# Hybrid decoder trunk on one core: the first layer's normalised input made from a second, already transposed copy of x

## The chip, the core and the metric

One Trainium2 chip, one core. The metric is the device time of one execution in microseconds. In the text, PE is TensorE, PEld its weight loads, DVE VectorE, ACT ScalarE, POOL GpSimd, and SP the engine whose queue issues most DMAs.

## What is computed

Two decoder layers on x, 256 tokens by 1024, batch 1. Each layer normalises x, projects it to ten groups of 512 columns, runs three branches on them (block attention, a gated linear recurrence, attention to 256 memory tokens), multiplies by a SiLU gate and adds the output projection to x.

```python
for l in range(DEPTH):                                   # 2
    h = rms_norm(x, norm_g[l])
    proj = h @ w_in[l]                                   # 1024 x 5120
    q_a, k_a, v_a, q_h, f_h, i_h, q_m, z = jnp.split(proj, split_points, axis=-1)
    qa, ka = rope(rms_norm(q_a)), rope(rms_norm(k_a))    # 8 heads x 64
    o_a = moba_attention(qa, ka, v_a)
    o_h = rms_norm(hgrn2_chunkwise(q_h, f_h, i_h, lb_all[l]), hgrn_o_norm[l])   # 4 heads x 128
    kv_m = rms_norm(mem, mem_norm_g[l]) @ w_mem_kv[l]
    k_m, v_m = jnp.split(kv_m, 2, axis=-1)
    o_m = memory_attention(rms_norm(q_m), rms_norm(k_m), v_m)                   # 4 heads x 128
    y = jnp.concatenate([o_a, o_h, o_m], axis=-1) * jax.nn.silu(z)
    x = x + y @ w_out[l]
```

## The kernel before

**Matmuls in three passes.** Each f32 operand is split into a high half (rounded to fp32r) and a low half (the rest), and a product is high x high, high x low and low x high. Weights come in chunks of 128 x 1024 from HBM, 60 per layer. For each chunk SP loads `wr`, ACT makes `wh` (L207 or L211) and DVE makes `wl` (L221 or L225); there are 4 buffers of `wr` and 3 each of `wh` and `wl`. Chunks 0 to 7 are the memory's keys and values, 8 to 11 the forget gates (one head of 128 columns each), 12 to 15 the recurrence's queries, 16 to 19 the attention's keys (KA), 20 to 23 the recurrence's input (IH), 24 to 27 the attention's queries (QA), and so on to the output projection.

**The normalised input.** The projections need x with its 1024 columns on the partitions: `hT`, eight tiles of 128 columns by 256 tokens, each with a high and a low half side by side (`hTh`, `hTl`). `g_norm` makes it: ACT squares the rows of `xs` with a sum, DVE and POOL turn the sum into a factor per token `r`, DVE scales the rows (`xn`, L473), PE transposes sixteen blocks of 128 x 128 (L481) into a side tile `sd`, and ACT and DVE take the halves out of it with the gain `gT` (L489, L490). For layer 0 this runs beside the memory's key and value matmuls (`group_kv`), whose operand `mT` comes from HBM in columns. `group_a` then computes the forget gates with `hT` as the moving operand; ACT copies the second half of the accumulator out as `al` and DVE adds it to the first as `as` (`g_sum`, L351 and L352).

**Work beside it in this stage.** `g_mem_r` squares the memory's rows (`memr`, L448) for its factor `rm`. `g_km` copies the key accumulators out as `kn` (DVE the first, ACT the second), ACT squares them (`sq`), DVE reduces the squares (L618), and POOL makes the factor `rk` after eight mask steps `mk` (L597) which need `xf`; `xf` lies in a buffer of `sq`. DVE then scales `kn` (L648). `g_vm` takes the value accumulators out as `vmh` (ACT) and `vml` (DVE). `g_setup` makes the rotation tables in many small DVE steps (`rt`), the last of which feeds one sine on ACT (`sc`, L561), behind a load of the sine's table. In the recurrence DVE computes `hQ` and ACT copies the last of it to `hQb` (L811). `g_ih` copies the IH accumulators out on ACT (L735).

**What sets the order.** Each piece of vector work is a generator that a `step()` per half chunk of matmuls moves on. From the recorded program a list scheduler with a timeline of its own sets the final order on each engine, fixed when the kernel is built; `tc.keep_in_program_order` and `tc.issue_after` hold an instruction in place. Accumulators have 4 buffers, side tiles 4.

Of the kernel before, what the change touches and what calls it, by code (L numbers as in the profile page):

```python
# [18 lines left out]
OP = mybir.AluOpType  # L19
# [25 lines left out]
@with_exitstack  # L45
def hymba_kernel(ctx: ExitStack, tc: tile.TileContext, x, mem, mem_t, positions, w_in, w_out, w_mem_kv,
                 gains, moba_g, out):
# [152 lines left out]
    def h_to(n):  # L200
        while st["h"] < min(n, len(chunks)):
            i = st["h"]
            whs[i] = sb.tile([128, 1024], F32R, name="wh", tag="wh", bufs=WH_BUFS)
            g = chunks[i][2]
            if g is None:
                with behind("ACT"):
                    nc.scalar.copy(whs[i], raws[i])  # L207
            else:
                for sl in parts(i):
                    with behind("ACT"):  # L210
                        nc.scalar.activation(whs[i][:, sl], raws[i][:, sl], AF.Copy, scale=gT[:, g:g + 1])  # L211
            st["h"] += 1

    def l_to(n):
        while st["l"] < min(n, len(chunks)):
            i = st["l"]
            wls[i] = sb.tile([128, 1024], F32R, name="wl", tag="wl", bufs=WL_BUFS)
            g = chunks[i][2]
            if g is None:
                with behind("DVE"):  # L220
                    nc.vector.tensor_tensor(wls[i], raws[i], whs[i].bitcast(F32), op=OP.subtract)  # L221
            else:
                for sl in parts(i):
                    with behind("DVE"):
                        ins = nc.vector.scalar_tensor_tensor(wls[i][:, sl], in0=raws[i][:, sl], scalar=gT[:, g:g + 1],  # L225
                                                             in1=whs[i][:, sl].bitcast(F32),
                                                             op0=OP.mult, op1=OP.subtract)
# [65 lines left out]
    def group_kv(th, tl, km, vm):  # L293

        acc = [[acc_tile() for _ in range(2)] for _ in range(2)]

        def part(c, g):
            i = c + c0
            wH, wL = whs[i][:, g * 512:(g + 1) * 512], wls[i][:, g * 512:(g + 1) * 512]
            for t in range(2):  # L300
                ts = slice(t * 128, (t + 1) * 128)
                mm(acc[g][t], th[:, c, ts], wH, c == 0, False)
                mm(acc[g][t], tl[:, c, ts], wH, False, False)
                mm(acc[g][t], th[:, c, ts], wL, False, c == 7)

# [12 lines left out]
        for c in (6, 7):  # L318
            part(c, 0)
            if c == 7:  # L320
                spawn(km(acc[0]))
            slot(False)
        for c in (6, 7):
            part(c, 1)
            fin()
            if c == 7:
                spawn(vm(acc[1]))
            slot(True)
# [116 lines left out]
    def g_mem_r():  # L445
        ss = small("ssm", 2)
        for t in range(2):
            nc.scalar.activation(memr[t], memr[t], AF.Square, accum_out=ss[:, t:t + 1])  # L448
        rel("P", 2)
# [10 lines left out]
    def g_norm(l):  # L460
# [10 lines left out]
        yield  # L471
        for t in range(2):
            nc.vector.tensor_scalar(xn[t], xs[:, t], r[:, t:t + 1], None, op0=OP.mult)  # L473
        yield 3
        for kp in range(4):
            yield from room("sd")
            pt = side_tile()
            for j in range(2):
                k = kp * 2 + j
                for t in range(2):  # L480
                    ins = nc.tensor.transpose(pt[:, j * 256 + t * 128:j * 256 + (t + 1) * 128],  # L481
                                              xn[t][:, k * 128:(k + 1) * 128], ident)
                    if l == 0:
                        tc.keep_in_program_order(ins)
            for j in range(2):
                k = kp * 2 + j
                c = GR_NORM + 8 * l + k
                src = pt[:, j * 256:(j + 1) * 256]
                nc.scalar.activation(hTh[:, k], src, AF.Copy, scale=gT[:, c:c + 1])  # L489
                nc.vector.scalar_tensor_tensor(hTl[:, k], in0=src, scalar=gT[:, c:c + 1],  # L490
                                               in1=hTh[:, k].bitcast(F32), op0=OP.mult, op1=OP.subtract)
# [123 lines left out]
    def sumsq(dst, acc, n):  # L615
        sq = sb.tile([128, 512], F32, name="sq", tag="sq", bufs=2)
        nc.scalar.activation(sq, acc, AF.Square)
        nc.vector.tensor_reduce(dst, heads(sq, n), AX.X, OP.add)  # L618
# [46 lines left out]
    def g_vm(l, acc):  # L665
# [4 lines left out]
        for t in range(2):  # L670
            nc.scalar.activation(vmh[:, t], acc[t], AF.Copy, scale=rm[:, t:t + 1])
            nc.vector.scalar_tensor_tensor(vml[:, t], in0=acc[t], scalar=rm[:, t:t + 1], in1=vmh[:, t].bitcast(F32),
                                           op0=OP.mult, op1=OP.subtract)
        T["vm"] = vmh, vml
# [692 lines left out]
```

## Time and profile before

| | us |
|---|---|
| median of 3 runs | 391.02 (390.81 to 393.14) |
| the profiled execution, device time | 390.31 |
| its span, first to last instruction | 388.5 |
| PE busy | 383.0 |
| DVE busy | 320.6 |
| ACT busy | 247.9 |
| POOL busy | 84.7 |
| granted TensorE clock | 0.999 |

The page gives busy times, the chain of work that ended last, and groups by line. In rows of the timeline the columns are the start in us from the span's start, the length in us of the merged row, the engine, line, operation, output<-inputs, shape, and how many instructions (xN); in brackets stands how long the engine was idle ahead of it and which instruction ended that. Matmuls are pipelined, so the next one starts before the last one's length is over; the cost of one is the step from start to start.

### The profile page before, as it was taken

What the parts mean: (1) busy time and instruction counts of PE and PEld (TensorE: products, weight loads), DVE (VectorE), ACT (ScalarE), POOL (GpSimd) and SP (SyncE); (2) the same over time, 40 slices, a digit from 0 to 9 for tenths busy, and PEclk for the clock granted to TensorE, in tenths of its full rate; (3) what the DMA queues carried; (4) which work ended last, traced back from release to release, by engine and by line L of the source; (5) the groups of instructions that cost most, each with busy time, mean ns of one, the idle gap of its engine ahead of it and who ended that gap; (6) DMA issues with size and microseconds to landing.
All of it is one profiled execution on the core that took longest, in us unless ns stands there. A gap on an engine that the chain in (4) does not pass through costs nothing.

```text
span 388.5 us, 6794 instructions
## 1 busy us (share of the span) xinstructions
PE 383.0 (99%) x2455; PEld 318.6 (82%) x2455; DVE 320.6 (83%) x621; ACT 247.9 (64%) x414; POOL 84.7 (22%) x129
## 2 busy tenths in 40 slices
PE   8999999999999999999999999999999999999996
PEld 5888887888788888778888888888888888877885
DVE  5789899999659999877576789899696799997663
ACT  5988755567768749473376666445765894885540
POOL 3014300525103523400000040014061063342000
PEclk9999999999999999999999999999999999999999
DMA  7986595539534999975454558636665189998512
GB/s 268 421 300 217 177 310 165 168 116 324 180 102 160 274 283 347 323 221 183 162 197 162 188 192 250 237 111 205 232 208 172 54 264 278 343 313 257 183 42 108
DMA packets 26241, 84.48 MB, mean 217 GB/s; under 512 B 3552, under 2 KB 5984, under 8 KB 26208
## 3 DMA queue, kind: packets, MB, share of 16 engines
q1 hardware_dynamic: 22304, 71.31, 55.1%
q0 software_dynamic: 3616, 12.59, 10.3%
q8 instruction: 19, 0.31, 0.3%
q10 hardware_dynamic: 288, 0.15, 0.1%
q14 instruction: 14, 0.11, 0.1%
HBM read 74.60 MB, written 9.44 MB: 216 GB/s over the span
## 4 chain that ended last, share of the span: by engine, by line
PE 97%; DMA 1%; DVE 0%; SPq 0%; ACT 0%; issue 0%; DVEq 0%
PE acc L268 69%; PE acc L1253 17%; PE sd L268 6%; PE sd L272 4%; DMA wr<-in_w_mem_kv_dram 1%; PE sd L481 1%; PE sd L1139 0%; PE sd L1009 0%; SPq L171 0%; ACT wh L211 0%; DVE xs L1287 0%; DVE xs L1294 0%; DVEq L1294 0%
## 5 line engine op out<-in xcount | busy, mean ns | idle before, releaser
L207 ACT CAST wh<-wr 128x1024 fp32r<-128x1024 f32 x96 | 100.8, 1051 | 69.3 <-PE acc L268 50.9
L221 DVE TENSOR_TENSOR wl<-wr,wh 128x1024 fp32r<-128x1024 f32 x96 | 116.8, 1217 | 26.2 <-ACT wh L207 26.0
L268 PE MATMUL acc<-wh,hT 128*128 128x512 f32 x384 | 122.9, 394 | 0.0
L268 PEld LDWEIGHTS acc<-wh,hT 128*128 128x128 f32 x384 | 71.5, 188 | 15.8 <-issue 0.7
L268 PE MATMUL acc<-wl,hT 128*128 128x512 f32 x192 | 75.6, 394 | 0.0
L268 PE MATMUL acc<-hT,wh 128*128 128x512 f32 x256 | 64.8, 392 | 0.0
L268 PEld LDWEIGHTS acc<-hT,wh 128*128 128x128 f32 x256 | 46.0, 189 | 8.5 <-ACT kn L631 0.4
L268 PEld LDWEIGHTS acc<-wl,hT 128*128 128x128 f32 x192 | 36.1, 188 | 7.3
L225 DVE SCALAR_TENSOR_TENSOR wl<-wr,gT,wh 128x1024 fp32r<-128x1024 f32 (+1 forms) x29 | 31.1, 1097 | 9.5 <-ACT wh L211 9.4
L1253 PE MATMUL acc<-wl,yh 128*128 128x512 f32 (+1 forms) x96 | 37.4, 390 | 0.0
L1253 PE MATMUL acc<-wh,yl 128*128 128x512 f32 (+1 forms) x96 | 37.2, 388 | 0.0
L268 PEld LDWEIGHTS acc<-hT,wl 128*128 128x128 f32 x256 | 34.9, 190 | 2.5
L211 ACT ACTIVATE wh<-wr,gT 128x1024 fp32r<-128x1024 f32 (+1 forms) x29 | 28.3, 1001 | 12.8 <-PE acc L1253 5.0
L268 PE MATMUL acc<-hT,wl 128*128 128x256 f32 x256 | 35.7, 282 | 0.0
L1253 PE MATMUL acc<-wh,yh 128*128 128x512 f32 (+1 forms) x96 | 33.6, 394 | 0.2
L268 PE MATMUL acc<-wh,mTh 128*128 128x512 f32 x64 | 25.0, 394 | 0.7 <-ACT mTh L422 0.4
L268 PE MATMUL acc<-wh,mTl 128*128 128x512 f32 x64 | 24.8, 390 | 0.0
L974 POOL TENSOR_TENSOR rka<-msa,pw 128x8 f32<-128x8 f32 x4 | 9.9, 2476 | 58.2 <-DVE msa L973 58.2
L1060 ACT ACTIVATE P<-P,nba,rq 128x128 f32<-128x128 f32 (+1 forms) x32 | 17.1, 536 | 8.3 <-DVE nba L1054 8.3
L1253 PEld LDWEIGHTS acc<-wh,yh 128*128 128x128 f32 x96 | 18.0, 188 | 5.0 <-issue 1.7
L1253 PEld LDWEIGHTS acc<-wl,yh 128*128 128x128 f32 x96 | 18.0, 188 | 4.0 <-DVE wl L225 0.7
L1253 PEld LDWEIGHTS acc<-wh,yl 128*128 128x128 f32 x96 | 18.0, 188 | 3.7
(219 smaller groups left out, 588.2 us busy)
## 6 DMA issues: line engine op xcount, KB each, us to landing
wr<-in_w_in_dram SPq DMA_DIRECT2D x80, 512.0 KB, 4.2
wr<-in_w_out_dram SPq DMA_DIRECT2D x24, 512.0 KB, 5.9
wr<-in_w_mem_kv_dram SPq DMA_DIRECT2D x15, 512.0 KB, 4.4
there<-blk POOLq DMA_DIRECT2D x4, 768.0 KB, 5.8
PT<-there POOLq DMA_DIRECT2D x16, 192.0 KB, 4.7
there<-blk POOLq DMA_DIRECT2D x6, 512.0 KB, 5.5
there<-blk SPq DMA_DIRECT2D x4, 512.0 KB, 2.8
P<-there POOLq DMA_DIRECT2D x16, 128.0 KB, 6.3
```

The lines of the kernel that those rows point to most:

```text
L207: nc.scalar.copy(whs[i], raws[i])
L211: nc.scalar.activation(whs[i][:, sl], raws[i][:, sl], AF.Copy, scale=gT[:, g:g + 1])
L221: nc.vector.tensor_tensor(wls[i], raws[i], whs[i].bitcast(F32), op=OP.subtract)
L225: ins = nc.vector.scalar_tensor_tensor(wls[i][:, sl], in0=raws[i][:, sl], scalar=gT[:, g:g + 1], in1=whs[i][:, sl].bitcast(F32), op0=OP.mu ...
L268: nc.tensor.matmul(o, lhsT=a, rhs=b, start=s, stop=e)
L272: tc.keep_in_program_order(nc.tensor.matmul(o, lhsT=a, rhs=b, start=s, stop=e))
L481: ins = nc.tensor.transpose(pt[:, j * 256 + t * 128:j * 256 + (t + 1) * 128], xn[t][:, k * 128:(k + 1) * 128], ident)
L974: nc.gpsimd.tensor_tensor(r[:, t8], ms[:, t8], pw[:, :8], op=OP.pow)
L1060: nc.scalar.activation(P[:, i, kc[t]], P[:, i, kc[t]], AF.Exp, bias=nb[:, c:c + 1], scale=rq[:, r:r + 1], accum_out=sm[:, c:c + 1])
L1253: ins = nc.tensor.matmul(a, lhsT=y, rhs=wt[:, cs], start=n == (0 if to is None else nk - 2) and j == 0, stop=n == nk - 1 and j == 2)
```

## The change

The host passes a second copy of x, `x_t`, in which each partition holds one column index and the tokens lie in strips of 32. It is loaded to a tile `xT` (128 x 2048), two DMAs of 512 KB. In layer 0 the factor `r` is spread along 128 columns (`rc`), two matmuls against the identity turn it into a row of factors on all partitions (`rb`), and DVE multiplies each of the eight column tiles of `xT` by gain and factor; ACT and DVE then take the high and low halves four tiles at a time. Layer 1 keeps the transposes. `xT` shares its memory with the two halves of the recurrence's gated output, which become one tile `y`. In `group_kv`, in both layers, the matmuls of the last two chunks are kept in program order, so the key accumulators end first. `in_turn` then chains instructions of layer 0 on DVE and on ACT.

```diff
+    def in_turn(*names):
+        for a, b in zip(names, names[1:]):
+            tc.add_manual_dep(N[b].ins, N[a].ins.name,
+                              mybir.DependencyInfo(mybir.DependencyClass.NoSync, mybir.DependencyReason.DATA),
+                              reason="in_turn")
...
-        def part(c, g):
+        def part(c, g, pinned=False):
...
-                mm(acc[g][t], th[:, c, ts], wH, c == 0, False)
-                mm(acc[g][t], tl[:, c, ts], wH, False, False)
-                mm(acc[g][t], th[:, c, ts], wL, False, c == 7)
+                for a, b in ((th, wH), (tl, wH), (th, wL)):
+                    ins = nc.tensor.matmul(acc[g][t], lhsT=a[:, c, ts], rhs=b, start=c == 0 and (a, b) == (th, wH),
+                                           stop=c == 7 and (a, b) == (th, wL))
+                    if pinned:
+                        tc.keep_in_program_order(ins)
...
         for c in (6, 7):
-            part(c, 0)
+            part(c, 0, True)
...
+    xT = sb.tile([128, 8, 8, 32], F32, name="xT", tag=f"y{H_}", bufs=1)
+    for t in range(2):
+        load(xT[:, 4 * t:4 * t + 4].rearrange("p q k i -> p (q k i)"),
+             dram(x_t, t * 128 * D, [[D, 128], [1, D]]))
     for t in range(2):
         load(memr[t], dram(mem, t * 128 * D, [[D, 128], [1, D]]))
...
+        if l == 0:
+            rc = sb.tile([128, 2, 128], F32, name="rc", tag="sq", bufs=2)
+            nc.vector.tensor_copy(rc, r[:, :, None].to_broadcast([128, 2, 128]))
+            yield 2
+            rb = side_tile()
+            for t in range(2):
+                mm_row(rb[:, t * 128:(t + 1) * 128], rc[:, t], ident)
+            rb3 = rb[:, :256].rearrange("p (q i) -> p q i", i=32)
+            yield
+            for k in range(8):
                 c = GR_NORM + 8 * l + k
+                N["xT", k] = nc.vector.scalar_tensor_tensor(xT[:, :, k], in0=xT[:, :, k], scalar=gT[:, c:c + 1], in1=rb3,
+                                                            op0=OP.mult, op1=OP.mult)
+                if k % 4 == 3:
+                    ks = slice(k - 3, k + 1)
+                    src = xT[:, :, ks].rearrange("p q k i -> p k q i")
+                    hi, lo = (a[:, ks].rearrange("p k (q i) -> p k q i", i=32) for a in (hTh, hTl))
+                    N["hTh", k // 4] = nc.scalar.copy(hi, src)
+                    N["hTl", k // 4] = nc.vector.tensor_tensor(lo, src, hi.bitcast(F32), op=OP.subtract)
             rel()
+        else:
...
         group_a(hT, lambda h, a: g_f(l, h, a))
+        if l == 0:
+            in_turn(*(("xT", k) for k in range(8)), ("hTl", 0), ("kn", 0), ("hTl", 1),
+                    ("wl", 8), ("wl", 9), ("vml", 0), ("vml", 1), ("wl", 10))
+            in_turn(("memr", 0), ("hTh", 0), ("hTh", 1), ("kn", 1), ("wh", 8), ("memr", 1), ("wh", 9),
+                    ("vmh", 0), ("vmh", 1), ("wh", 10), ("knsq", 0))
...
+    def strips(a):
+        return a.reshape(2, 4, 32, 8, 128).transpose(0, 4, 1, 3, 2)
...
+        "x": v["x"], "x_t": strips(v["x"]), "mem": v["mem"], "mem_t": columns(v["mem"]).reshape(128, 4, 512).transpose(1, 0, 2),
```

The scheduler moves other instructions as well. First the DMA queue of SP at the start, before and after:

```order
L171 DMA wr<-in_w_mem_kv_dram 128x1024 x3
L171 DMA memr<-in_mem_dram 128x1024 x2
L171 DMA wr<-in_w_in_dram 128x1024 x4
L171 DMA pos_i<-in_positions_dram 128x2
L171 DMA mg<-in_moba_g_dram 128x256
```

```order
L179 DMA wr<-in_w_mem_kv_dram 128x1024 x3
L179 DMA xT<-in_x_t_dram 128x1024 x2
L179 DMA memr<-in_mem_dram 128x1024 x2
L179 DMA wr<-in_w_in_dram 128x1024 x3
L179 DMA pos_i<-in_positions_dram 128x2
L179 DMA mg<-in_moba_g_dram 128x256
```

The two loads of `xT` stand ahead of the memory's rows, and one weight load fewer stands ahead of the positions.

Next DVE while the first forget gates run, up to the reduction of the memory keys' squares (`ssk`):

```order
L221 TENSOR_TENSOR wl<-wr,wh 128x1024
L521 CAST pf<-pos_i 128x2
L672 SCALAR_TENSOR_TENSOR vml<-acc,rm,vmh 128x512
L221 TENSOR_TENSOR wl<-wr,wh 128x1024
L524 TENSOR_TENSOR rt<-pf,fr 128x16
L672 SCALAR_TENSOR_TENSOR vml<-acc,rm,vmh 128x512
L618 TENSOR_REDUCE ssk<-sq 128x4 x2
```

```order
L362 TENSOR_TENSOR as<-acc,al 128x256
L566 TENSOR_SCALAR rt<-rt 128x16
L567 TENSOR_SCALAR rt<-rt 128x16
L572 SCALAR_TENSOR_TENSOR rt<-rt 128x16 x2
L706 SCALAR_TENSOR_TENSOR vml<-acc,rm,vmh 128x512
L565 TENSOR_SCALAR rt<-rt 128x16
L706 SCALAR_TENSOR_TENSOR vml<-acc,rm,vmh 128x512
L566 TENSOR_SCALAR rt<-rt 128x16
L229 TENSOR_TENSOR wl<-wr,wh 128x1024
L567 TENSOR_SCALAR rt<-rt 128x16
L651 TENSOR_REDUCE ssk<-sq 128x4 x2
```

Before, the reduction follows the second `vml` at once, behind the `wl` of the second and third gate heads; now the first head's sum `as` and four steps of the rotation tables stand ahead of the first `vml`, and the `wl` of the third head between the second `vml` and the reduction.

Last ACT at the end of the IH group, ahead of the copies of its accumulators (`ih`):

```order
L207 CAST wh<-wr 128x1024 x2
L811 COPY hQb<-hQ 128x16x32
L207 CAST wh<-wr 128x1024
L561 ACT_TABLE_LOAD
L561 ACTIVATE sc_164<-rt 128x32
L735 COPY ih<-acc 128x512
```

```order
L215 CAST wh<-wr 128x1024 x2
L849 COPY hQb<-hQ 128x16x32
L594 ACT_TABLE_LOAD
L594 ACTIVATE sc_167<-rt 128x32
L215 CAST wh<-wr 128x1024
L769 COPY ih<-acc 128x512
```

The table load and the sine stand ahead of the weight's cast now; the copy `ih` still comes behind all three.

More of the change, by code (lines that the diff above doesn't have):

```diff
@@ L45, in hymba_kernel @@
 @with_exitstack
-def hymba_kernel(ctx: ExitStack, tc: tile.TileContext, x, mem, mem_t, positions, w_in, w_out, w_mem_kv,
+def hymba_kernel(ctx: ExitStack, tc: tile.TileContext, x, x_t, mem, mem_t, positions, w_in, w_out, w_mem_kv,
                  gains, moba_g, out):
@@ L206, in h_to @@
                 with behind("ACT"):
-                    nc.scalar.copy(whs[i], raws[i])
+                    N["wh", i] = nc.scalar.copy(whs[i], raws[i])
             else:
@@ L447, in g_mem_r @@
         for t in range(2):
-            nc.scalar.activation(memr[t], memr[t], AF.Square, accum_out=ss[:, t:t + 1])
+            N["memr", t] = nc.scalar.activation(memr[t], memr[t], AF.Square, accum_out=ss[:, t:t + 1])
         rel("P", 2)
@@ L616, in sumsq @@
         sq = sb.tile([128, 512], F32, name="sq", tag="sq", bufs=2)
-        nc.scalar.activation(sq, acc, AF.Square)
+        N["sq"] = nc.scalar.activation(sq, acc, AF.Square)
         nc.vector.tensor_reduce(dst, heads(sq, n), AX.X, OP.add)
@@ L629, in g_km @@
         kn = sb.tile([128, 2, 512], F32, name="kn", tag="qk", bufs=1)
-        nc.vector.tensor_copy(kn[:, 0], acc[0])
-        nc.scalar.copy(kn[:, 1], acc[1])
+        N["kn", 0] = nc.vector.tensor_copy(kn[:, 0], acc[0])
+        N["kn", 1] = nc.scalar.copy(kn[:, 1], acc[1])
         yield
@@ L670, in g_vm @@
         for t in range(2):
-            nc.scalar.activation(vmh[:, t], acc[t], AF.Copy, scale=rm[:, t:t + 1])
-            nc.vector.scalar_tensor_tensor(vml[:, t], in0=acc[t], scalar=rm[:, t:t + 1], in1=vmh[:, t].bitcast(F32),
-                                           op0=OP.mult, op1=OP.subtract)
+            N["vmh", t] = nc.scalar.activation(vmh[:, t], acc[t], AF.Copy, scale=rm[:, t:t + 1])
+            N["vml", t] = nc.vector.scalar_tensor_tensor(vml[:, t], in0=acc[t], scalar=rm[:, t:t + 1],
+                                                         in1=vmh[:, t].bitcast(F32), op0=OP.mult, op1=OP.subtract)
         T["vm"] = vmh, vml
@@ L766, in y_tiles @@
         if f"y{br}" not in T:
-            T[f"y{br}"] = [sb.tile([128, 4, 256], F32R, name=f"y{c}{br}", tag=f"y{c}{br}", bufs=1) for c in "hl"]
+            if br == H_:
+                y = sb.tile([128, 2, 4, 256], F32R, name=f"y{br}", tag=f"y{br}", bufs=1)
+                T[f"y{br}"] = [y[:, 0], y[:, 1]]
+            else:
+                T[f"y{br}"] = [sb.tile([128, 4, 256], F32R, name=f"y{c}{br}", tag=f"y{c}{br}", bufs=1) for c in "hl"]
         return T[f"y{br}"]
@@ L1348 @@
     laid = {
-        "x": v["x"], "mem": v["mem"], "mem_t": columns(v["mem"]).reshape(128, 4, 512).transpose(1, 0, 2),
+        "x": v["x"], "x_t": strips(v["x"]), "mem": v["mem"], "mem_t": columns(v["mem"]).reshape(128, 4, 512).transpose(1, 0, 2),
         "positions": v["positions"].reshape(2, 128).T,
```

50 lines of the change are left out of this document (26 added, 24 removed).

## The prediction

> **What bounds the kernel now.** The share of busy time comes first, then the chain that ended last.
>
> ```profile
> span 388.5 us, 6794 instructions
> PE 383.0 (99%) x2455; PEld 318.6 (82%) x2455; DVE 320.6 (83%) x621; ACT 247.9 (64%) x414; POOL 84.7 (22%) x129
> PE 97%; DMA 1%; DVE 0%; SPq 0%; ACT 0%; issue 0%; DVEq 0%
> ```
>
> PE works 383.0 of 388.5 us, and 97% of the chain is PE. Next I ask who makes PE wait; the answer is three rows, all in the first 7 us.
>
> ```profile
> PE sd L268 <- DVE dm L396: 1.0, 1, 1.0
> PE acc L268 <- ACT mTh L422: 0.4, 1, 0.4
> PE acc L268 <- ACT wh L211: 0.3, 1, 0.3
> ```
>
> So from then until the output leaves, PE never stands still. Any matmul taken out shortens the run by its own length, but only if every operand is ready that much sooner. An engine that has no slack at one place turns the gain into a wait there, and PE never makes up a wait. Which engine has no slack? The stretches say VectorE (columns: stretch and length, then busy time and instructions of PE, PEld, DVE, ACT, POOL, then clock, DMA share, GB/s).
>
> ```profile
> 60.00:70.00 10.00, 10.00 (x165) 7.91 (x164) 10.00 (x33) 5.00 (x7) 0.70 (x1) 1.00 0.42 136
> 100.00:120.00 20.00, 20.00 (x119) 16.26 (x118) 12.97 (x48) 15.55 (x32) 0.00 (x0) 1.00 0.35 116
> ```
>
> DVE is busy all of the 10 us from 60 to 70, and 12.97 of 20 us after 100. What is late must be late before 100.
>
> **The change on PE.** The sixteen transposes of layer 0 stand here:
>
> ```profile
> 21.77 1.03 PE L481 MATMUL sd<-ident,xn 128*128 128x128 f32 x8
> 22.56 0.71 PE L268 MATMUL acc<-wl,mTh 128*128 128x512 f32 x2
> 23.11 1.04 PE L481 MATMUL sd<-ident,xn 128*128 128x128 f32 x8
> 23.90 0.47 PE L268 MATMUL acc<-wh,mTh 128*128 128x512 f32 x1
> 24.21 0.39 PE L268 MATMUL acc<-wh,mTl 128*128 128x512 f32 x1
> 24.44 0.39 PE L268 MATMUL acc<-wh,mTh 128*128 128x512 f32 x1
> ```
>
> An ordinary matmul follows the last by 0.23 us (24.21 to 24.44). From 21.77 to 24.21 there are three of them, 0.68 us, so the transposes take 2.44 - 0.68 = 1.76 us. The two matmuls that spread the factor (rb) have no row. Bounds: the same shape as a transpose, 0.10 us each (21.77 to 22.56 for eight), or at most an ordinary 512-column one, 0.23 us. The nearest are plain matmuls of f32 tiles, 128x128:
>
> ```profile
> 110.41 1.27 PE L268 MATMUL sd<-ih,hST 128*128 128x128 f32 x10
> 111.52 0.39 PE L268 MATMUL sd<-ih,hX 128*128 128x128 f32 x2
> ```
>
> Ten in 1.11 us, 0.11 each; I take 0.22 for the pair. **PE's work falls by 1.54 us** (1.30 to 1.56).
>
> [...]
>
> **The head of the forget gates.** They begin at 29.46; without the 1.54 at 27.92. Can the columns be ready?
>
> ```profile
> 14.63 0.90 SPq L171 DMA_DIRECT2D memr<-in_mem_dram x2
> DMA to landing us min/median/max: 6.0/6.4/6.8
> 17.98 1.42 DVE L473 TENSOR_SCALAR xn<-xs,rx 128x1024 f32<-128x1024 f32 x2 [0.84 <-POOL rx L470]
> 19.31 3.67 DVE L225 SCALAR_TENSOR_TENSOR wl<-wr,gT,wh 128x1024 fp32r<-128x1024 f32 x3
> 25.77 1.26 DVE L490 SCALAR_TENSOR_TENSOR hT<-sd,gT,hT 128x256 fp32r<-128x256 f32 x3
> 28.51 0.89 POOL L574 COPY rtA<-mg 128x96 f32<-128x96 f32 x4 [2.27 <-DMA mg<-in_moba_g_dram]
> 29.46 3.59 PE L268 MATMUL acc<-hT,wh 128*128 128x512 f32 x15
> ```
>
> SP now issues the two xT loads where the memr loads stood. Those landed at 20.6 (14.63 + 6.0) and 21.9 (15.1 + 6.8), 1.3 us a load; xT should land then, and memr and the first gate weights 2.6 us later. DVE's scaling of xn (1.42) becomes a spread copy of about 0.3 us (an estimate from the 0.42 of a 256-column op in the row of three), so the three wl end 1.1 us sooner, at 21.9, just as xT is there. Eight products follow. Bounds for one: 0.31, a quarter of a wl (3.67 / 3 / 4), and 0.63, a 512-column reduction (a row below). I take the nearest, 0.42, a product of the same size that reads PSUM: the last ends at 25.3. The eight lower halves from PSUM give way to two of about 1.15 each. ACT, held to squaring the first memr (lands at 23.2) ahead of the upper halves, has time for it before 25.3; then the second upper half (about 1.0, as a wh), kn (0.5, as ih below) and the first head's wh bring it to 27.8. PE may start at 27.9: no wait, but no slack either. POOL's rm now queues behind three rtA copies that wait for mg; those started at 28.5 and take 0.2 each, and rm's input, behind the second memr square on ACT, comes at about 29.4: no cost, but an mg that is 1 us later would hold vmh and the third head's wh.
>
> **Then the order costs.** Vector work that PE's first head must end for now stands ahead of the memory keys' reduction.
>
> ```profile
> 35.03 2.00 PE L268 MATMUL acc<-hT,wh 128*128 128x512 f32 x8
> 36.87 1.11 PE L268 MATMUL acc<-hT,wl 128*128 128x256 f32 x8
> 37.82 2.00 PE L268 MATMUL acc<-hT,wh 128*128 128x512 f32 x8
> 34.04 0.37 ACT L351 COPY al<-acc 128x256 f32<-128x256 f32 x1
> 29.30 0.74 ACT L671 ACTIVATE vmh<-acc,rm 128x512 fp32r<-128x512 f32 x1
> 31.05 0.74 DVE L672 SCALAR_TENSOR_TENSOR vml<-acc,rm,vmh 128x512 fp32r<-128x512 f32 x1
> 33.59 1.27 DVE L618 TENSOR_REDUCE ssk<-sq 128x4 f32<-128x512 f32 x2
> 34.33 0.27 POOL L594 CAST xf<-ti 128x96 f32<-128x96 int32 x1 [4.93 <-DVE ssk L618]
> 41.67 1.50 DVE L648 TENSOR_TENSOR kn<-kn,rk 128x512 f32<-128x512 f32 x2 [1.81 <-POOL rk L645]
> 72.17 0.66 DVE L887 TENSOR_TENSOR hQ<-hQ,hT 128x512 f32<-128x512 f32 x1
> ```
>
> A head takes 2.79 us (35.03 to 37.82), so the first ends at 30.7. ACT, held at its al with both vmh and the third head's wh queued behind, goes on at 30.9; DVE does as, five small steps and two vml (0.67 each), then wl at 33.9 and the first reduction to 35.8, where it ended at 34.2. POOL's xf waits for that reduction, then come mk and rk on POOL: kn followed xf by 7.34 us (41.67 - 34.33) and now starts at about 43.15, 1.5 late, with DVE waiting about 2 us for it. From there to hQ DVE ran 31.16 us without a gap (to 72.83). Its list is the same but for the small rt steps, 28 before and 21 after, since seven went into the wait. Alone such a step takes about 0.08, chained 0.2; I take 1.6 off (bounds 0 and 2). hQ then ends at 43.15 + 29.55 = 72.7: **no earlier than the 72.83 of before.**
>
> **Who waits for hQ.**
>
> ```profile
> 72.92 0.62 ACT L811 COPY hQb<-hQ 128x512 f32<-128x512 f32 x1 [1.45 <-DVE hQ L887]
> 73.44 1.05 ACT L207 CAST wh<-wr 128x1024 fp32r<-128x1024 f32 x1
> 74.51 1.28 ACT L561 ACT_TABLE_LOAD   x1
> 75.80 0.23 ACT L561 ACTIVATE sc<-rt 128x32 f32<-128x32 f32 x1
> 75.94 0.57 ACT L735 COPY ih<-acc 128x512 f32<-128x512 f32 x1
> 75.75 0.89 PE L272 MATMUL sd<-hQ,hK 128*32 128x48 f32 x64
> 76.57 0.50 PE L268 MATMUL acc<-wh,hT 128*128 128x512 f32 x1
> ```
>
> PE's QA group starts at 76.57, in the accumulator that ih's copy frees at 76.51: no slack, though no wait shows. ACT takes 3.02 us from hQb to ih, and the new order holds the same work between them: table load and sc first, wh after. So ih ends at 72.75 + 3.02 + 0.57 = 76.3, while PE would be there at 76.57 - 1.54 = 75.03. It waits some 1.2 to 1.3 us. Net gain: 1.54 - 1.25 = **0.3 us**. Behind it I see nothing new: what follows starts from PE's place, and DVE has 7 free us in 100 to 120. The changed order of layer 1 and the joined y tile I cost at nothing: no row of DVE or ACT held PE in that layer (the three waits above are all there are), and the group pieces that are now in a fixed order are as many as before. If that cover is gone, it costs the rest of one wl, at most 1.2 us.
>
> [...]
>
> **The rivals.** (1) **The gain stays whole**, 391.02 - 1.54 = 389.5: it needs hQ at 71.3, kn at 41.8. For it: DVE's 2 us wait for rk goes if POOL runs mk sooner. Against: mk stands behind the reduction and that behind wl and vml. (2) **Slower: the columns land late.** If the xT loads come with memr or the gate weights instead of ahead of them, by 2.5 us, products end at 27.8, gates start at 30.2 for 27.92, reduction and kn come 2.3 later, QA at 78.6: +2.0, 393.0. It decides from a landing after 22.0, each us costing one; +0.3 is already slower than before. For: DMA is saturated there. Against: the memr loads landed in the order of issue. (3) **The table load holds ACT twice**: it now follows hQb directly, and if that costs its 1.28 us again, QA starts 1.3 later, 392.0. The 0.01 us from the end of the load to sc in the row above speak against it. [...] (4) **The change does not do what it says**: the spread factor cannot cost back its 1.76 by the rows above.
>
> **How the numbers follow.** The profiled run took 390.31 us, 1.8 around its span; the median is 391.02. 0.3 off gives 390.0 and, by the median, **390.7**. Chances: this forecast (390.1 to 391.3) 0.53, rival 1 0.22, rival 2 0.16, rival 3 0.03, other waits 0.06. Leaving rt at its full length (hQ at 74.3) gives 392.3, inside. Low end 389.3 for rival 1; high end 392.5 cuts the worse half of rival 2. One per cent, what a measurement here can tell from no change, is 3.9 us: neither the whole saving nor rival 2 reaches it, so same 0.95; 0.02 faster, 0.03 slower for a landing 4 us late.
>
> **What would show it.** L481 with 16 matmuls instead of 32, two rb; the gates starting near 27.9; kn's products near 43 behind rk; and a PE wait of about 1.2 us by ACT ih at the start of QA, near 76.3. No such wait and QA at 75.0 is rival 1. A DVE wait for xT's DMA and gates after 29 is rival 2. The forecast is wrong if DVE reaches hQ over half a us away from 72.7.

## The result, and the profile after

The changed kernel is slower, by 0.6%. Eight runs of each on one chip: 394.02 us median (392.02 to 395.56) against 391.12 us for the kernel before (390.21 to 393.14); the ratio is 1.0061, with a 95% interval of 1.0033 to 1.0089. The forecast was 390.7, in a range of 389.3 to 392.5.

The profiled execution took 395.56 us, the longest of the eight, with a span of 393.8 us; TensorE's mean granted clock in it is 0.996. In two of the eight runs that clock was 1.0, and they took 392.02 and 392.62; in the other six it was 0.994 to 0.996, and they took 393.75 to 395.56. So there are two things to find: what costs one or two microseconds in every run, and what the clock has to do with the rest.

PE's own waits of the changed kernel, summed by what it waited for (total, times, longest):

```profile
PE acc L276 <- ACT ih L769: 2.4, 1, 2.4
PE acc L276 <- ACT wh L215: 1.7, 3, 1.0
PE sd L276 <- DVE dm L410: 1.0, 1, 1.0
PE acc L311 <- ACT mTh L436: 0.4, 1, 0.4
PE acc L1291 <- DVE as L362: 0.3, 1, 0.3
```

Before there were three waits, all in the first 7 us. Now one of 2.4 us stands where the prediction put one of 1.25, at the copy of ih, and there are four smaller ones that it did not have. PE's timeline shows where (start, length, then the idle time ahead):

```profile
19.53 0.60 PE L280 MATMUL sd<-ident,rc 128*128 128x128 f32 x4
28.69 2.13 PE L276 MATMUL acc<-hT,wh 128*128 128x512 f32 x8 [0.38 <-ACT wh L215]
34.86 2.11 PE L276 MATMUL acc<-hT,wh 128*128 128x512 f32 x8 [0.30 <-ACT wh L215]
51.71 0.40 PE L276 MATMUL acc<-wh,hT 128*128 128x512 f32 x1
75.67 0.89 PE L280 MATMUL sd<-hQ,hK 128*32 128x48 f32 x64
78.95 0.50 PE L276 MATMUL acc<-wh,hT 128*128 128x512 f32 x1 [2.40 <-ACT ih L769]
80.22 1.23 PE L276 MATMUL acc<-wh,hT 128*128 128x512 f32 x3
88.92 0.72 PE L276 MATMUL acc<-wh,hT 128*128 128x512 f32 x2
157.84 2.11 PE L276 MATMUL acc<-hT,wh 128*128 128x512 f32 x8 [0.97 <-ACT wh L215]
```

And the row of the kernel before that answers to the one at 88.92, from its own timeline (the row at 76.57, where QA starts, stands in the prediction):

```profile
84.92 0.73 PE L268 MATMUL acc<-wh,hT 128*128 128x512 f32 x2
```

Row against row this gives PE's lead or lag: the gates start 0.77 us earlier (28.69 for 29.46), the keys' group at 51.71 only 0.08 earlier (51.79 before), QA 2.38 later (78.95 for 76.57), and the row behind QA 4.00 later (88.92 for 84.92). Between those last two PE has no wait, and still loses 1.62 us. The row at 80.22 shows how: three matmuls take 1.23 us where such a row of three took 0.84 elsewhere. One microsecond per line (busy time and number of instructions of PE, PEld, DVE, ACT, POOL; then the granted clock, the DMA share and GB/s):

```profile
80.00:81.00 1.00, 1.00 (x5) 0.83 (x4) 1.00 (x3) 0.34 (x1) 1.00 (x2) 0.74 0.00 0
81.00:82.00 1.00, 1.00 (x4) 0.81 (x3) 0.72 (x5) 0.00 (x0) 1.00 (x5) 0.50 0.00 0
82.00:83.00 1.00, 1.00 (x4) 0.71 (x4) 1.00 (x3) 0.00 (x0) 0.04 (x1) 0.50 0.78 176
83.00:84.00 1.00, 1.00 (x4) 0.81 (x3) 1.00 (x2) 0.38 (x1) 0.00 (x0) 0.55 0.83 328
```

The clock is halved from about 80.5 to 83.9, which by the column's values costs 0.26 + 0.50 + 0.50 + 0.45 = 1.7 us of TensorE's work, and it begins 1.5 us behind the end of the 2.4 us wait. The remaining 1.3 of the profiled run's 5.3 us are the wait of 0.97 at 157.84 and one of 0.29 behind it; ahead of the first, ACT had waited 3.1 us (until 149.2) for a weight load that took 7.7 us to land. In the later profiles of the changed kernel with an edit the first wait is 0.30 us (e3) or not there, and one of 0.3 like the second stands in e13 too, which has nothing of the change; so neither is counted as part of it.

Who made ih late? The rows from the head of the gates to ih, POOL, DVE and ACT apart, in order of time:

```profile
29.52 1.43 POOL L607 COPY rtA<-mg 128x96 f32<-128x96 f32 x3 [11.37 <-DMA mg<-in_moba_g_dram]
30.91 1.66 POOL L466 TENSOR_TENSOR rm<-msm,pw 128x2 f32<-128x2 f32 x1
36.81 0.27 POOL L627 CAST xf<-ti 128x96 f32<-128x96 int32 x1 [4.01 <-DVE ssk L651]
37.17 5.30 POOL L630 TENSOR_SCALAR mk<-xf 128x32 uint8<-128x32 f32 x8
42.44 1.66 POOL L677 TENSOR_TENSOR rk<-msk,pw 128x8 f32<-128x8 f32 x1
...
32.21 0.42 DVE L362 TENSOR_TENSOR as<-acc,al 128x256 f32<-128x256 f32 x1
34.85 1.22 DVE L229 TENSOR_TENSOR wl<-wr,wh 128x1024 fp32r<-128x1024 f32 x1
36.06 1.27 DVE L651 TENSOR_REDUCE ssk<-sq 128x4 f32<-128x512 f32 x2
44.55 1.50 DVE L682 TENSOR_TENSOR kn<-kn,rk 128x512 f32<-128x512 f32 x2 [2.54 <-POOL rk L679]
56.02 1.23 DVE L229 TENSOR_TENSOR wl<-wr,wh 128x1024 fp32r<-128x1024 f32 x1 [1.03 <-ACT wh L215]
74.57 0.66 DVE L925 TENSOR_TENSOR hQ<-hQ,hT 128x512 f32<-128x512 f32 x1
...
24.18 1.07 ACT L462 ACTIVATE memr<-memr 128x1024 f32<-128x1024 f32 x1 [3.26 <-DMA memr<-in_mem_dram]
31.81 0.37 ACT L361 COPY al<-acc 128x256 f32<-128x256 f32 x1 [1.18 <-PE acc L276]
32.61 1.26 ACT L705 ACTIVATE vmh<-acc,rm 128x512 fp32r<-128x512 f32 x2 [0.43 <-POOL rm L466]
54.93 1.06 ACT L215 CAST wh<-wr 128x1024 fp32r<-128x1024 f32 x1 [1.67 <-DMA wr<-in_w_in_dram]
75.32 0.62 ACT L849 COPY hQb<-hQ 128x512 f32<-128x512 f32 x1 [3.93 <-DVE hQ L925]
78.32 0.58 ACT L769 COPY ih<-acc 128x512 f32<-128x512 f32 x1
```

Read it as a chain with two beginnings. POOL's copies wait for mg, a load of 128 KB, until 29.5, and rm stands behind three of them: it ends at 32.57. ACT's vmh waits 0.43 us for rm, and behind vmh stand the wh of the third head and the squares. The other beginning is the first head: ACT's al waits 1.18 us for its accumulator, and DVE's `as` (32.21) follows al. From `as` on DVE goes through four small steps, two vml and wl10, the third head's wl (34.85), to the reductions (36.06) and shows no idle time; so by these rows an earlier rm, with every order as it is, would have moved little on DVE. POOL's xf waits for the first reduction (it sits in a buffer of the squares), eight masks follow, then rk; DVE waits 2.54 us for that and starts kn at 44.55. hQ ends at 75.23, ih at 78.90, and QA's first matmul at 78.95 needs the accumulator that ih frees.

By the order of the queue the extra loads stand at the top of the first beginning. Issue to landing of mg alone, after and then before, and of the two memr loads after:

```profile
DMA to landing us min/median/max: 7.6/7.6/7.6
```

```profile
DMA to landing us min/median/max: 4.1/4.1/4.1
```

```profile
DMA to landing us min/median/max: 8.4/8.8/9.1
```

mg was issued 2.5 us earlier than before (at 21.84, before at 24.39) and landed 1.0 us later, with the 1 MB of xT more and one weight load of 0.5 MB less ahead of it. That it is late because of them is argued from this order; no run takes the loads out.

### The profile page after: what moved, and what is told of

Its sections match the earlier page's. It is cut to its first block, busy times and chain, and to the rows that moved or that the text cites. A ratio compares the mean times of both kernels' runs of the same rounds, so it can differ in the third digit from the quotient of the medians.

```text
span 393.8 us, 6763 instructions
## 1 busy us (share of the span) xinstructions
PE 384.2 (98%) x2443; PEld 318.7 (81%) x2443; DVE 321.3 (82%) x622; ACT 246.5 (63%) x408; POOL 86.7 (22%) x129
## 4 chain that ended last, share of the span: by engine, by line
PE 78%; DMA 7%; DVE 7%; ACT 4%; issue 2%; POOL 1%; SPq 0%; ACTq 0%; DVEq 0%
PE acc L276 46%; PE acc L1291 17%; PE acc L311 6%; PE sd L276 5%; PE sd L280 3%; DMA wr<-in_w_mem_kv_dram 3%; DMA wr<-in_w_in_dram 2%; DMA mg<-in_moba_g_dram 2%; DVE wl L229 1%; ACT P L1216 1%; ACT wh L215 1%; DVE P L1106 1%; ACT wh L219 1%; DVE wl L233 1%; DVE zh L995 1%
## 5 line engine op out<-in xcount | busy, mean ns | idle before, releaser
L229 DVE TENSOR_TENSOR wl<-wr,wh 128x1024 fp32r<-128x1024 f32 x96 | 117.0, 1219 | 28.8 <-ACT wh L215 28.7
L276 PE MATMUL acc<-wh,hT 128*128 128x512 f32 x384 | 124.4, 398 | 2.4 <-ACT ih L769 2.4
L276 PEld LDWEIGHTS acc<-wh,hT 128*128 128x128 f32 x384 | 72.3, 190 | 18.6 <-ACT ih L769 2.5
L1012 POOL TENSOR_TENSOR rka<-msa,pw 128x8 f32<-128x8 f32 x4 | 10.8, 2711 | 65.2 <-DVE msa L1011 65.2
L1291 PE MATMUL acc<-wh,yl 128*128 128x512 f32 (+1 forms) x64 | 24.7, 386 | 0.0
L1291 PE MATMUL acc<-wl,yh 128*128 128x512 f32 (+1 forms) x64 | 24.7, 386 | 0.0
L1291 PE MATMUL acc<-wh,y 128*128 128x512 f32 x64 | 21.6, 403 | 0.4 <-DVE as L362 0.3
L1291 PE MATMUL acc<-wh,yh 128*128 128x512 f32 (+1 forms) x64 | 21.8, 386 | 0.0
L311 PE MATMUL acc<-wl,mTh 128*128 128x512 f32 x64 | 20.8, 391 | 0.0
L1012 POOL TENSOR_TENSOR rqa<-msa,pw 128x8 f32<-128x8 f32 x4 | 12.0, 3000 | 31.8 <-DVE msa L1011 31.8
```

The costliest lines, as they stand in the source:

```text
L229: N["wl", i] = nc.vector.tensor_tensor(wls[i], raws[i], whs[i].bitcast(F32), op=OP.subtract)
L276: nc.tensor.matmul(o, lhsT=a, rhs=b, start=s, stop=e)
L311: ins = nc.tensor.matmul(acc[g][t], lhsT=a[:, c, ts], rhs=b, start=c == 0 and (a, b) == (th, wH), stop=c == 7 and (a, b) == (th, wL))
L1012: nc.gpsimd.tensor_tensor(r[:, t8], ms[:, t8], pw[:, :8], op=OP.pow)
L1291: ins = nc.tensor.matmul(a, lhsT=y, rhs=wt[:, cs], start=n == (0 if to is None else nk - 2) and j == 0, stop=n == nk - 1 and j == 2)
```

## Experiments

My theory (A in the expectations) is the chain from mg and rm on; the rival B is named in each. Each group ran on one chip beside the kernel before, whose medians there were 390.62 (e1 to e4), 390.99 (e5 to e8), 390.82 (e9 to e11) and 390.97 us (e12 to e14). Each ratio is to the kernel before.

### 1 to 4: cut the chain at four places

Masks ahead of everything (e1), no held orders (e2), ih ahead of a weight's cast (e3), rm ahead of the copies that wait for mg (e4), each on the changed kernel alone:

```
e1  -    xf = sb.tile([128, 3, 32], F32, name="xf", tag="sq", bufs=2)
    +    xf = cst.tile([128, 3, 32], F32, name="xf")
e2  -        if l == 0:
    -            in_turn(*(("xT", k) for k in range(8)), ...)
    -            in_turn(("memr", 0), ("hTh", 0), ...)
e3  +        if l == 0 and gen is g_zh:
    +            in_turn(("ih", 0, 0), ("wh", 25))
e4  -        nc.gpsimd.tensor_tensor(rm, ms, pw[:, :2], op=OP.pow)
    +        N["rm"] = nc.gpsimd.tensor_tensor(rm, ms, pw[:, :2], op=OP.pow)
    ...
    -                nc.gpsimd.tensor_copy(A[:, :, 16:64], gb(16, 48))
    +                N["rtA", l, q] = nc.gpsimd.tensor_copy(A[:, :, 16:64], gb(16, 48))
    +                in_turn("rm", ("rtA", l, q))
```

> xf in a tile of its own, so that POOL makes the masks before 17 us; the orders of DVE, ACT, PE and SP are those of the changed kernel row for row, only POOL's xf and mk move ahead. Theory A (hQ is late because rk stands on POOL behind xf and eight mk, and these behind the late reduction): the DVE wait of 2.54 us for rk goes, kn at 42.0 instead of 44.55, hQ ends near 72.6, ih near 76.3, PE starts QA at 76.5 without a wait, and the stretch of half clock behind it (80.5 to 83.7, 1.6 us) goes with the wait: 394.0 - 2.4 - 1.6 = 390.0. Theory B (DVE itself is late, by the orders and by the wh that waited for a wr load): kn comes earlier but hQ still ends after 74.5, PE still waits over 1.5 us, 393 or more.

Measured: 390.32 us, ratio 0.9987 (0.9972 to 1.0002), clock 0.998 to 1.0 in all ten runs. Its rows (kn, ih and QA's first matmul):

```profile
42.45 1.50 DVE L682 TENSOR_TENSOR kn<-kn,rk 128x512 f32<-128x512 f32 x2
76.15 0.58 ACT L769 COPY ih<-acc 128x512 f32<-128x512 f32 x1
76.94 0.50 PE L276 MATMUL acc<-wh,hT 128*128 128x512 f32 x1
```

The wait for rk is gone, ih ends at 76.73, PE does not wait at QA and the half clock is gone with the wait. Nothing but the place of nine POOL instructions differs from the changed kernel, so some 2.9 us of its time hung on them (0.0074 between the two ratios to the kernel before). Theory A holds: kn, hQ, ih and the time came within half a us of its numbers. It holds for the part behind the reductions; rm and the reductions are no earlier in this run (33.04 and 36.52) than in the changed kernel.

> The two lists of held orders are left out, all else as changed. Theory A (the orders set the reduction behind wl10, and with it rk and hQ): the reductions end before 33, kn before 40, no wait at QA; PE instead waits for the wl and wh of the first gate heads, 1 to 3 us between 28 and 37; 391 to 393. Theory B (the orders are not the cause, the loads are): the wait for ih at QA stays over 2 us, 394 or more.

Measured: 395.28 us, ratio 1.0105 (1.0079 to 1.0131). Where PE's wait is:

```profile
33.70 5.31 PE L276 MATMUL acc<-hT,wh 128*128 128x512 f32 x16 [3.91 <-ACT wh L215]
```

My time for this run was wrong by 2 to 4 us. The planner (the list scheduler), left alone, puts both memr squares and the squares and reductions of the keys among and ahead of what the first head needs, the gates start at 33.7 instead of 28.7, and the clock was 0.990 to 0.996 in all four runs. At QA there is no wait. So the gates need held orders at their head; what these cost comes further down.

> The wh of the second QA chunk (1.03 us on ACT) is held behind ih's first copy. Both theories: ih 1.0 us earlier, PE waits 1.4 us instead of 2.4 at QA. If any wait of that size halves the clock behind it: 393.0. If the clock falls only for a longer wait: no stretch at half clock, 391.4.

Measured: 394.67 us, ratio 1.0091 (1.0067 to 1.0114), clock 0.999 to 1.0 in all four runs. A miss in time, for a reason that the timeline shows:

```profile
78.19 0.50 PE L276 MATMUL acc<-wh,hT 128*128 128x512 f32 x1 [1.62 <-ACT ih L769]
80.97 0.50 PE L276 MATMUL acc<-wh,hT 128*128 128x512 f32 x1 [1.13 <-DVE tm L1019]
```

The wait at ih shrank to 1.62 us, and the clock did not fall behind it; but PE then waited 1.13 us for DVE's tm, a rotation step of the keys whose end frees another accumulator, and 0.65 us further on for DVE's hKb, an operand of the recurrence. Neither is the cast that was pushed back: DVE was late as a whole (hQ at 75.40), and one earlier copy only passes the wait along.

> POOL's rm is held ahead of the four rtA copies that wait for mg. Theory A (mg, 1 us late behind the added loads, holds rm, vmh, wh10, wl10 and the reductions): rm ends near 31.2 instead of 32.57, vmh starts near 31.3, the waits of PE at the third head (0.3 us and the 0.5 beside it) go, reductions and kn come 1.3 us earlier, PE waits about 1.1 us for ih: 391.3 without a fall of the clock, 392.7 with it. Theory B: rm earlier moves nothing behind 35 us, 394.

Measured: 389.59 us, ratio 0.9977 (0.9963 to 0.9991): faster than the kernel before. All of PE's waits in it:

```profile
PE sd L276 <- DVE dm L410: 1.0, 1, 1.0
PE acc L311 <- ACT mTh L436: 0.6, 1, 0.6
PE acc L276 <- ACT wh L215: 0.5, 1, 0.5
```

rm now ends at 31.0, kn starts at 42.81, hQ ends at 73.29, and no wait is left from the third head on. My time for it, 391.3, was 1.7 us too long, because more than rm moved. With its new times the planner put ACT's al behind vmh, where it had stood ahead:

```profile
31.04 1.26 ACT L706 ACTIVATE vmh<-acc,rm 128x512 fp32r<-128x512 f32 x2 [0.66 <-POOL rm L466]
34.18 0.37 ACT L361 COPY al<-acc 128x256 f32<-128x256 f32 x1
```

On DVE `as` and the four small steps no longer stand ahead of the first vml, and `as` follows the reductions; and it put the table load behind ih's first copy, which takes 1.28 us out of ACT's way there. So e4 shows that rm's place with the order that follows from it is enough; how much is rm itself and how much the order, no run tells apart. At the far end e1 (with the table load where it was) shows that the earlier hQ alone is enough.

### 5, 6 and 9: the same lateness in the kernel before

The kernel before, with masks written twice, so that POOL reaches rk later:

```
-            nc.gpsimd.tensor_scalar(mk[:, j], xf[:, q], float(least), None, op0=OP.is_ge)
+            for _ in range(2 if j < 2 else 1):     # e5; j < 4 in e6, j < 8 in e9
+                nc.gpsimd.tensor_scalar(mk[:, j], xf[:, q], float(least), None, op0=OP.is_ge)
```

> The kernel before, with two of the eight masks written twice (1.22 us more on POOL ahead of rk), every other engine's order untouched. Theory A (kn behind rk sets hQ, hQ sets ih, and PE has no slack at QA): kn starts 1.2 us later, near 42.9, and PE waits 1.0 to 1.3 us for ih at QA; no fall of the clock, since a wait of 1.62 brought none: 390.6 + 1.2 = 391.8. Theory B (the loss of the changed kernel comes from its loads and orders, not from rk): 390.6.

> The kernel before, with four of the eight masks written twice (2.44 us more on POOL ahead of rk); the order differs in some rt steps and one pair on ACT, and nothing of the change is in it. Theory A: kn near 44.1, hQ ends near 75.0, PE waits 2.0 to 2.4 us for ih at QA, and in most runs the clock is halved for 3.3 us behind it, as in the changed kernel: 390.6 + 2.2 + 1.6 = 394.4, or 392.8 in a run without the fall. Theory B: 390.6 to 391.

> The kernel before, with all eight masks written twice; six of the eight extra writes stand ahead of rk (3.7 us by the mean of a mask in before). The run with four extra ones put kn only 1.6 us later. Theory A: kn near 45, hQ ends near 76, PE waits 2 to 3 us for ih at QA. If a wait of that size halves TensorE's clock for a stretch behind it: clock 0.996 in most runs and 390.8 + 2.8 + 1.6 = 395; if the half clock in the changed kernel had another cause: clock 0.999 and 393.6.

Measured: 391.42 us, 1.0008 (0.9995 to 1.0022); 391.63 us, 1.0016 (1.0001 to 1.0031); 391.57 us, 1.0007 (0.9981 to 1.0032). QA's first matmul in the three:

```profile
77.67 0.50 PE L268 MATMUL acc<-wh,hT 128*128 128x512 f32 x1 [0.40 <-ACT ih L736]
```

```profile
77.94 0.50 PE L268 MATMUL acc<-wh,hT 128*128 128x512 f32 x1 [0.90 <-ACT ih L736]
```

```profile
77.98 0.50 PE L268 MATMUL acc<-wh,hT 128*128 128x512 f32 x1 [1.31 <-ACT ih L736]
```

The wait appears where theory A says, with nothing of the change in the program, and grows. Its size was overestimated: an extra mask costs POOL about 0.25 us, not the mean of 0.61 (14 of them took 6.37 us, against 4.89 for 8). Counted from the first gate (30.10, 29.87 and 29.49 in the three, 29.46 before), kn came 0.5, 1.2 and 2.1 us later, not 1.2, 2.4 and 3.7. By the times alone only e6 is told from no change. The test of the clock that e9 was meant for failed: its wait was too short.

### 7 and 8: is there more to gain?

Both edits of e1 and e4 together (e7); and with them the first memr square held behind the upper halves and wh8 instead of ahead of them (e8):

```
e8  -            in_turn(("memr", 0), ("hTh", 0), ("hTh", 1), ("kn", 1), ("wh", 8), ("memr", 1), ("wh", 9),
    +            in_turn(("hTh", 0), ("hTh", 1), ("kn", 1), ("wh", 8), ("memr", 0), ("memr", 1), ("wh", 9),
```

> rm ahead of the rtA copies and xf in its own tile, both. Theory A: PE has no wait at QA with the first alone, so that an earlier rk has nothing left to give: 389.6, as with rm alone, within 0.4. Theory B (each takes off its own share): 388 or less.

> As the run with both, and the first memr square is held behind both upper halves and wh8 instead of ahead of them, so that ACT needn't wait 3.5 us for memr. The upper halves start at 24.0 instead of 25.0, wh8 ends near 27.6, and the gates start at PE's own pace, 28.1, without the 0.45 us wait: 389.2. If memr's square comes so late that rm and with it vmh and wh10 are late again: PE waits 0.5 us or more at the third head, 389.7 or more.

Measured: 389.54 us, 0.9963 (0.9942 to 0.9984), and 389.31 us, 0.9955 (0.9934 to 0.9976). As theory A has it, an earlier rk has nothing left to give once PE has no wait at QA: 389.54 beside e4's 389.59. e8 is the fastest median of all, 1.7 us ahead of the kernel before in the same session; that it beats e7 is not shown, the intervals overlap.

### 10 and 11: the two other parts of the orders

On e4, the last pieces of the keys' and values' group left to the planner again (e10); on the changed kernel, both lists cut off behind wl9 and wh9 (e11):

```
e10 -            part(c, 0, True)
    +            part(c, 0)
    -            part(c, 1, True)
    +            part(c, 1)
e11 -                    ("wl", 8), ("wl", 9), ("vml", 0), ("vml", 1), ("wl", 10))
    +                    ("wl", 8), ("wl", 9))
    -                    ("vmh", 0), ("vmh", 1), ("wh", 10), ("knsq", 0))
```

> rm ahead of the rtA copies, and the group pieces of chunks 6 and 7 of the keys and values are left to the planner again (layer 0's last pieces and layer 1's). If the fixed order costs nothing, as the prediction had it: 389.6, as with rm alone, within 0.4. If it costs: 389 or less; if it gains: 390.2 or more.

> The changed kernel with the two lists cut off behind wl9 and wh9, so that the keys' squares and reductions no longer stand behind vmh, vml and the third head's wh and wl. Theory A (the tail of the lists makes the reductions late, and rm's lateness comes in only through it): reductions end near 34.5 instead of 37.3, kn starts before 42, no wait at QA; PE waits at the second or third head for wh or wl, 0.5 to 1.5 us: 390.5 to 391.5. Theory B (the lists' tail is not what holds the reductions): kn stays after 44, PE waits over 2 us at QA, 394.

Measured: e10 391.05 us, 1.0020 (1.0000 to 1.0040), 1.3 us above e4 when each median is taken against the kernel before beside it; e11 390.26 us, 0.9974 (0.9958 to 0.9990). PE at the first gate of e10, then kn in e11:

```profile
29.83 2.11 PE L276 MATMUL acc<-hT,wh 128*128 128x512 f32 x8 [1.17 <-ACT wh L215]
```

```profile
39.35 1.51 DVE L682 TENSOR_TENSOR kn<-kn,rk 128x512 f32<-128x512 f32 x2 [0.88 <-POOL rk L679]
```

The fixed order of the last pieces is no side issue: without it the keys' accumulator is done later, ACT's copy kn, which the held order puts ahead of wh8, starts at 28.25 instead of 26.87, and the gates start at 29.83 where e4 has 28.44. In e11 the reductions ran at 29.8 and 30.6, kn at 39.35, and behind 28 us PE waits only 0.27 us at the third head and 0.17 at the output projection; the time is a little below the expected range. mg and the extra loads are as in the changed kernel, and rm still stands behind the copies. So what put the reductions, and with them rk and hQ, late is the lists' tail, which sets them behind vml and the third head's wl; the lists' head is what helps.

### 12 to 14: does a wait alone halve the clock?

The kernel before, where QA's first matmul waits also for one later instruction: wl26 (e12), ih's second copy (e13) or wh26 (e14):

```
+    def hold(a, b):
+        tc.add_manual_dep(a.ins, b.ins.name,
+                          mybir.DependencyInfo(mybir.DependencyClass.Sync, mybir.DependencyReason.DATA),
+                          reason="hold")
...
+                if l == 0 and gen is g_zh:
+                    hold(M["qa"], M["wl", 26])     # e13: M["ih", 0, 1]; e14: M["wh", 26]
```

> The kernel before, where QA's first matmul also waits for wl26, which ends at 79.3 in its trace; the program has nothing of the change. PE idles 2.7 us at 76.6. Theory A (such a wait halves the clock behind it): a stretch of about 3.3 us at 0.5, clock 0.996 or less in most runs, 390.8 + 2.7 + 1.6 = 395.1. Rival (the half clock of the changed kernel had another cause, or chance): clock 0.998 to 1.0 and 393.5.

> The same, but QA's first matmul waits for ih's second copy (ends at 77.95): a wait of 1.4 us. By the runs with waits of 1.3 and 1.6 us, whose clocks were 0.998 to 1.0, no fall: 390.8 + 1.4 = 392.2. If the length doesn't matter: 0.996 and 393.8.

> The same with wh26 (ends at 77.46): a wait of 0.9 us, every engine's order as before. No fall of the clock, 390.8 + 0.9 = 391.7; where later slack takes the wait up again, 391.

Measured: e12 394.78 us, 1.0104 (1.0060 to 1.0147), clocks 0.996, 1.0, 0.996, 0.989; e13 392.44 us, 1.0040 (1.0024 to 1.0056), seven runs at 0.998 to 1.0; e14 391.93 us, 1.0027 (1.0009 to 1.0044), nine of ten at 0.998 to 1.0. QA in e12, and its clock a microsecond at a time:

```profile
79.03 0.79 PE L275 MATMUL acc<-wh,hT 128*128 128x512 f32 x1 [2.93 <-DVE wl L228]
```

```profile
79.00:80.00 1.00, 0.97 (x2) 0.83 (x3) 0.56 (x5) 0.00 (x0) 0.93 (x6) 0.53 0.05 16
80.00:81.00 1.00, 1.00 (x4) 0.76 (x3) 1.00 (x3) 0.04 (x1) 0.00 (x0) 0.50 0.95 270
81.00:82.00 1.00, 1.00 (x4) 0.81 (x3) 1.00 (x4) 0.57 (x1) 0.00 (x0) 0.50 0.59 238
82.00:83.00 1.00, 1.00 (x4) 0.79 (x4) 1.00 (x4) 0.00 (x0) 0.00 (x0) 0.76 0.00 0
```

A wait of 2.9 us, with nothing else changed on the way to it, brings the same stretch at half clock; its one run at full clock took 393.55, the others 394.38 to 397.34. Waits of 1.46 and 1.05 us cost their own length (1.5 and 1.0 us) and no more. So a wait alone can bring the half clock, at 2.9 us; that one of 2.4 does is shown by the changed kernel beside e1, which has neither the wait nor the half clock in ten runs.

## Why the prediction was wrong, point by point

The mechanism was the right one, from hQ through ih to QA. The step that failed is the time of hQ, 43.15 + 29.55 = 72.7: it was 2.5 us too early, and the prediction's own sign for a wrong forecast (half a us away) was met. Besides, the price of a wait lacked a term.

| step | predicted | measured |
|---|---|---|
| pair of rb matmuls | 0.22 us | 0.36 (19.53 to 19.89), four records |
| last product of the columns ends | 25.3 | 25.4 |
| second upper half, then wh8 end | 26.3, 27.8 | 27.2, 28.6 |
| gates start | 27.92 | 28.69 |
| rm ends | about 30.1 (input 29.4, 0.70) | 32.57 (input 30.5, start 30.91, 1.66) |
| wl10 starts | 33.9 | 34.85 |
| xf to kn on POOL | 7.34 | 7.74 |
| kn starts | 43.15 | 44.55 |
| kn to the end of hQ | 29.55 | 30.68, of it 1.03 waiting for a weight load |
| hQ ends | 72.7 | 75.23 |
| hQb's start to ih's end | 3.59 | 3.58 |
| PE's wait at QA | 1.25 | 2.40 |
| clock behind it | not in the sum | half for 3.4 us, 1.7 us |

**What held.** The columns themselves landed and were scaled as forecast. The order from hQb to ih costs what the rows of before said, to 0.01 us, and the table load cost its 1.28 us once and nothing beside it (the row of ih at 78.32 follows hQb at 75.32 by 3.00; 3.02 before), so rival 3 fell. The filling of DVE's wait with rotation steps saved what was claimed: kn to hQ without the 1.03 us wait is 29.65. PE waited for ih at QA, as named.

**hQ, in three parts.** First, the reductions: wl10 started 0.95 us after the forecast, and xf 1.0 us (36.81 for the 35.8 at which the first reduction was to end). DVE shows no idle time from `as` to there, and `as` waited for the first head, which began 0.77 us late: memr landed at 24.1, not 23.2, and the upper halves stood behind its square. So the 0.8 us at the head, which cost PE its lead, also moved the reductions. Second, POOL from xf to kn took 0.4 longer than the row of before. Third, the stretch from kn to hQ, which DVE ran without a gap before, has waits for weight casts that the sum put at nothing: 1.03 us at 56.02, from a weight load that SP issues behind the keys' turn, and so behind kn. An earlier kn does not take such waits away: DVE's waits in this stretch add up to 0.81 us in e1 and 0.91 in e4.

**rm at no cost** is a sentence of the prediction that failed too. Its condition was named (an mg that is 1 us later would hold vmh and the third head's wh), and the sum went without it. mg did land 1.0 us later, at 29.5, and rm ended 2.5 us behind its forecast. Of these, 1.1 are rm's input, which DVE made only at 30.3 to 30.5, behind the first head's wl; 0.4 are the copies, 1.43 us for an expected 0.6; and 1.0 is rm itself, 1.66 for 0.70. In the trace it costs ACT 0.43 us and PE a wait of 0.30 at the third head. That its place also decides the planner's order ahead of the reductions is what e4 shows, and e11 shows that with a shorter list the same mg costs nothing at QA. I had weighed the extra loads for the columns (rival 2) and had not carried the same lateness to mg, which comes behind them.

**PE's lead.** With the 0.77 us at the head, of which 0.14 is the dearer rb pair, the wait at the third head and 0.11 to 0.13 to get going again behind each wait (the rows of eight matmuls at 28.69 and 34.86 took 1.97 and 1.95 us to the next row, those without a wait 1.84), PE's 1.5 us were spent by 52 us. PE's own lateness changed no time by itself: with PE earlier, the wait at QA would have been longer.

**The price of a wait** is a term that was not there: a wait on PE was priced at its length. Near the forecast's 1.25 us that held: e13's wait of 1.46 us cost 1.5, e14's of 1.05 cost 1.0. At 2.4 it did not. In the profiled run a wait of twice the forecast length cost more than three times as much with the half clock behind it, and that took its time past the upper end of the range.

**Costed at nothing and not nothing:** the fixed order of the group's last pieces gains about 1.3 us (e10 against e4). The forecast of 27.92 for the gates took for granted that the key accumulators end in time; it was luck that this needed no term, because without the fixed order they don't. The joined y tile and layer 1 showed no wait of their own in e4, e7 and e8.

For the sum at the median: 394.02 less 391.12 is 2.9 us. The wait at QA with the half clock gives 2.4 + 1.6 in the profiled run; two of the eight runs were spared the half clock, and with 392.02 and 392.62 they lie 0.9 and 1.5 us above the median of before, less than a wait of 2.4. No trace tells how long the wait was in the runs that were not profiled. How much of the median is each part is therefore open, while both are shown as causes by e1 and e12.

## What to carry to other kernels

When a change adds loads to a queue, follow every transfer behind them to the instruction that waits for it, and then look at what is queued behind that instruction on its engine: here a 128 KB load that was 1 us late stood ahead of a two-column operation on POOL, and with that operation ahead of it, and the order that the planner then chose, the wait on TensorE 50 us on was gone. Look whether an engine that was busy without a gap stays so when its inputs move. Hold in a fixed order only what the next matmul needs, and keep work that waits for nothing (the masks) ahead of what waits; one buffer shared with a late tile had put it behind. Don't price a wait on TensorE at its length alone: in this kernel waits of 1.05 to 1.62 us left the clock at 1.0, while behind one of 2.40 us the stretch at half clock cost 1.6 us more, two thirds of the wait again.

## What the runs showed of the hardware that I had not expected

**The clock fell behind a wait of 2.4 us.** Traced waits of 1.05 (e14), 1.31 (e9), 1.46 (e13) and 1.62 us (e3) in a stream of dense matmuls left the granted clock at 1.0; 2.40 us (the changed kernel) and 2.93 us (e12) were followed by some 3.4 us at 0.5 (80.5 to 83.9 and 79.1 to 82.5), starting 1.5 us after the end of the first and at the end of the second. Behind e2's wait of 3.91 us sixteen matmuls took 5.14 us (33.70 to 38.84) where rows of eight took 1.84 further on, so 1.46 us more. What a wait between 1.62 and 2.40 us does, none of these profiles shows. Over runs, the mean clock was 0.996 or less in six of eight with the first, three of four with the second, all four of e2 with its 3.9 us, and now and then without such a wait in the profile (three of ten runs of e7, four of the 87 of the kernel before that ran beside the experiments). Why the clock falls in some runs and not in others, the traces do not show.

**POOL beside a running weight operation on DVE.** rm took 0.69 to 0.70 us in the profiles of before, e4, e7, e8, e10 and e11, where no wl was running on DVE when it began, and 1.66 us in after, e1 and e3, where it began 0.16 or 0.17 us after one. In after, DVE's wl ran from 30.75 to 32.02 and rm from 30.91 to 32.57; in all three rm ended 0.55 or 0.56 us after that wl. rk's first step is alike: 2.63 us in e1 and 2.72 in e11, where it began 0.09 and 0.03 us after a wl, and 1.66 or 1.67 in before, after, e2, e3, e4, e9 and e10, where none was running when it began. In e4 and e7 a wl began 0.14 and 0.16 us after rm, and rm took 0.69; in e9 one began 0.81 us after rk, and rk took 1.67. Whether the wl is the cause, no run isolates.

**A plain f32 matmul of 128 columns stood as two records.** The code's two spread matmuls stand as four in the trace, 0.09 us apart, so the pair costs 0.36 where two transposes cost 0.22 (1.76 for the sixteen). The prediction's ten in 1.11 us were records too, and so five matmuls: the code of before has 16 products of ih and hST, and its trace 32. Read so, that row would have given 0.44 for the pair. By these figures a plain matmul cost 1.6 times a transpose here.
